# One trunk layer of a hybrid diffusion backbone: the ConvFFN's up projection with seven products of halves in place of eight

## The chip, the cores and the metric

The kernel runs on one core of a Trainium2 chip. The metric is the time of one execution in device microseconds (us). TensorE (PE) multiplies matrices and writes to PSUM, eight banks of 512 fp32 columns; VectorE (DVE), ScalarE (ACT) and GpSimd (POOL) work element by element, POOL on SBUF tiles only in this kernel; SyncE (SP) issues nearly all DMA transfers. Every engine takes its instructions in the order of its own queue, and semaphores hold an instruction until its operands and its buffer are ready.

## The reference

The layer takes a prompt of 128 tokens and 512 latent tokens, width 1,024, through norm, modulation, two kinds of attention and the ConvFFN, with a sandwich of norms around each. The change lies in the ConvFFN:

```python
def conv_ffn(h, w_up, conv_w, conv_b, w_down):
    u = h @ w_up
    up = jnp.pad(u, ((0, 0), (1, 1), (0, 0)))
    u = up[:, :-2] * conv_w[0] + up[:, 1:-1] * conv_w[1] + up[:, 2:] * conv_w[2] + conv_b
    gate, val = jnp.split(u, 2, axis=-1)
    return (jax.nn.silu(gate) * val) @ w_down
```

`w_up` is 1,024 x 5,632 (2,816 gate columns, then 2,816 value columns), `w_down` 2,816 x 1,024. Everything is fp32. The convolution runs along the tokens, over the 128 prompt tokens and the 512 latent ones apart.

## The kernel before

**Precision.** Every matrix product is made of three fp32r matmuls: each operand is split into a high part (a copy to fp32r on ScalarE, `act`, line 107) and a low part (the rest, a subtraction on VectorE, `tt`, line 110), and `mm3` (line 128) adds high x high, high x low and low x high into the same PSUM bank. `split` (121) does both steps for one tile.

**Units.** The 5,632 columns are cut into 22 units of 128 gate and 128 value columns (`NF`, line 20). `wtile` (532) loads one 1,024 x 128 block of weights (512 KB) as 8 blocks of 128 rows and splits it. The 640 tokens lie in `h2H` and `h2L` (two tiles each, four blocks of 128 channels per tile) with columns of zeros between the sequences, 644 columns in all (`TO`, 1291).

**Up.** For each unit, each of gate and value (`gv`) and each of two chunks of 322 and 324 token columns (`CH`, 1410), `up_mm` (1416) accumulates 8 x 3 = 24 matmuls into one bank: 96 matmuls for a unit. `up_ev` (1436) makes the convolution straight from the bank: a scaled copy with bias on ScalarE (middle tap), and two taps on VectorE (`stt`, line 118). `up_act` (1450) applies silu on ScalarE and multiplies gate by value on VectorE into `aT`, six SBUF tiles that hold all activations, 22 x 642 columns.

**What orders the work.** Up to line 1572 the order in each engine's queue is the order of the code (`manual_schedule`, from 1462; an earlier such region ends at line 1186). That part holds the out projection of attention, block by block of 128 tokens (`p_mm`, `p_y`, `p_sq`, `p_z`, `p_r`, `p_x`, `p_sx`, `p_n`, lines 1324 to 1356), the transposed and modulated input of the FFN (`p_T`, `p_h`, `p_s`, 1361 to 1390), the last modulation columns as filler for TensorE (`tick`, 1476, with loads `wms` on SP's queue), and the first chunk of units 0 and 1 (`up_mm(0, 0, 0)` to `up_ev(1, 1, 0)`, with weights `wu` split early). From 1573 on a scheduler at compile time orders the instructions; it may queue them ahead of hand-ordered ones.

**Down.** For each half of the 1,024 output columns, eleven steps (1622) load 256 rows of `w_down` (512 KB) and split them, split two units of `aT` into `aH` and `aL`, and add into five PSUM banks, one for each block of 128 tokens: 2 x 5 x 3 = 30 matmuls of 512 columns. `fin` (1606) closes a block with its norm and writes the output.

**Buffers.** SBUF tiles come from pools with a fixed number of buffers: `u` (10 large ones), `ws0` and `ws1` (one each, raw weights), `wh` and `wl` (two each, split weights), `pt` (6), `q` (2), `fp` (2), `p` (9). A tile waits until the last reader of the buffer's former tile is done.

## Time and profile before

| what | value |
|---|---|
| median of 3 runs | 869.59 us (866.78 to 872.27) |
| the profiled execution's own time | 876.65 us |
| span of its instructions | 874.9 us |
| up projection, units 2 to 21 | 428.7 to 714.8 us |
| down projection and output | 714.8 to 874.9 us |
| mean granted TensorE clock | 0.983 |

Times in rows of the profile are in us from the start of the span. A row of a group gives line, engine, operation, the tiles written and read (out<-in), their shapes and the count, then the busy time in us and the mean of one in ns, then the idle time of the engine just before these instructions and what ended it. A row of the timeline gives start and duration in us, and in brackets the idle time before. A row of the busy time by stretch gives for each engine the busy us and the count in that stretch, the granted clock, the DMA engines' mean busy share and GB/s. The line of an instruction is that of the helper that records it (107, 110, 119, 126), so tiles tell them apart.

### The profile page before, as it was taken

Reading aid. Unit: us, or ns where it says so; the run is one execution under the profiler, and the core shown is the slowest. Engines: PE = TensorE matmul, PEld = TensorE weight load, DVE = VectorE, ACT = ScalarE, POOL = GpSimd, SP = SyncE. Lnnn points to the kernel's source line nnn. Section 1 sums busy time; section 2 is a strip of 40 time slices with the busy share of each in tenths; the row PEclk is TensorE's granted clock in tenths of the full one; section 3 lists DMA queues with packets and bytes.
Section 4 is the critical chain, followed back from the end, with each engine's and each line's share of the span. In section 5 each row is a group of like instructions: output and inputs, shape, how many; then the busy total and the mean of one; then the engine's idle time right before and its main releaser. Section 6 shows DMA issues by size and latency. Waiting matters only on the chain.

```text
span 874.9 us, 14025 instructions
## 1 busy us (share of the span) xinstructions
PE 833.2 (95%) x5496; PEld 737.6 (84%) x5496; DVE 485.8 (56%) x1044; ACT 410.0 (47%) x829; POOL 129.9 (15%) x259
## 2 busy tenths in 40 slices
PE   2998999999999999999999999999999999999997
PEld 2767878888788778769999999999999998888885
DVE  1533556655788874577555555555555463427315
ACT  3433567645578885567433333333333352327112
POOL 1434143423231211142000000000000000000002
PEclk9989899999999998999999999999999999999999
DMA  6996555462622021644122222222222222222213
GB/s 134 256 246 110 142 145 145 117 172 76 151 73 72 27 73 37 208 146 121 49 73 73 73 73 73 73 73 76 80 83 76 73 71 75 73 72 73 85 60 120
DMA packets 136679, 88.09 MB, mean 101 GB/s; under 512 B 15753, under 2 KB 124581, under 8 KB 136613
## 3 DMA queue, kind: packets, MB, share of 16 engines
q1 hardware_dynamic: 135604, 86.54, 34.8%
q8 instruction: 43, 0.70, 0.3%
q10 hardware_dynamic: 1008, 0.66, 0.2%
q14 instruction: 24, 0.19, 0.1%
HBM read 83.16 MB, written 4.51 MB: 100 GB/s over the span
## 4 chain that ended last, share of the span: by engine, by line
PE 78%; DMA 7%; DVE 5%; ACT 5%; SPq 2%; issue 1%; POOL 1%; DVEq 0%; POOLq 0%; ACTq 0%
PE psu L126 36%; PE psd L126 18%; PE psg L126 9%; PE psya L126 3%; DMA wm<-in_w_mod_dram 2%; PE psS L126 2%; PE psO L126 2%; PE psyb L126 2%; ACT P L107 1%; PE psv L126 1%; PE psT L720 1%; DMA wms<-in_w_mod_dram 1%; DMA xs<-in_x_sample_dram 1%; PE psg L382 1%; SPq L233 1%
## 5 line engine op out<-in xcount | busy, mean ns | idle before, releaser
L126 PE MATMUL psu<-h2H,wh 128*128 128x322 f32 (+1 forms) x672 | 208.9, 311 | 0.0
L126 PE MATMUL psu<-h2H,wl 128*128 128x322 f32 (+1 forms) x672 | 208.8, 311 | 0.0
L126 PE MATMUL psu<-h2L,wh 128*128 128x322 f32 (+1 forms) x672 | 208.2, 310 | 0.0
L126 PEld LDWEIGHTS psu<-h2H,wh 128*128 128x128 f32 x672 | 127.1, 189 | 0.2 <-issue 0.2
L126 PEld LDWEIGHTS psu<-h2L,wh 128*128 128x128 f32 x672 | 127.0, 189 | 0.0
L126 PEld LDWEIGHTS psu<-h2H,wl 128*128 128x128 f32 x672 | 126.6, 188 | 0.0
L119 DVE SCALAR_TENSOR_TENSOR cv<-psu,T,cv 128x322 f32<-128x322 f32 (+1 forms) x176 | 96.6, 550 | 37.9 <-ACT cv L107 33.5
L107 ACT ACTIVATE wh<-wst 128x1024 fp32r<-128x1024 f32 x56 | 59.4, 1060 | 118.5 <-PE psu L126 55.2
L110 DVE TENSOR_TENSOR wl<-wst,wh 128x1024 fp32r<-128x1024 f32 (+1 forms) x45 | 54.6, 1214 | 101.4 <-ACT wh L107 101.2
L126 PE MATMUL psd<-wdl,aH 128*128 128x512 f32 x220 | 86.9, 395 | 0.0
L126 PE MATMUL psd<-wdh,aL 128*128 128x512 f32 x220 | 86.6, 394 | 0.0
L126 PE MATMUL psd<-wdh,aH 128*128 128x512 f32 x220 | 86.6, 394 | 0.0
L126 PE MATMUL psg<-hH,wh 128*128 128x320 f32 x224 | 77.4, 345 | 6.7 <-ACT T L107 3.1
L107 ACT ACTIVATE cv<-psu,T 128x320 f32<-128x320 f32 (+1 forms) x88 | 53.2, 607 | 45.5 <-PE psu L126 45.5
L126 PE MATMUL psg<-hH,wl 128*128 128x320 f32 x224 | 71.2, 318 | 0.0
L126 PE MATMUL psg<-hL,wh 128*128 128x320 f32 x224 | 71.2, 318 | 0.0
L116 POOL TENSOR_SCALAR rdv<-ssdc 128x1 f32<-128x1 f32 x5 | 1.9, 383 | 459.1 <-ACT jk L107 459.1
L126 PEld LDWEIGHTS psg<-hH,wh 128*128 128x128 f32 x224 | 44.0, 196 | 16.1 <-ACT T L107 7.0
L110 DVE TENSOR_TENSOR aL<-aT,aH 128x1284 fp32r<-128x1284 f32 x22 | 32.6, 1492 | 37.3 <-ACT aH L107 29.3
L110 DVE TENSOR_TENSOR wdl<-wd,wdh 128x1024 fp32r<-128x1024 f32 x22 | 26.9, 1222 | 47.2 <-ACT wdh L107 47.2
L107 ACT ACTIVATE wdh<-wd 128x1024 fp32r<-128x1024 f32 x22 | 23.2, 1055 | 61.2 <-PE psd L126 55.6
L126 PEld LDWEIGHTS psd<-wdl,aH 128*128 128x128 f32 x220 | 41.4, 188 | 9.9 <-DVE wdl L110 0.3
(277 smaller groups left out, 1513.5 us busy)
## 6 DMA issues: line engine op xcount, KB each, us to landing
wst<-in_w_up_dram SPq DMA_DIRECT2D x44, 512.0 KB
wms<-in_w_mod_dram SPq DMA_DIRECT2D x32, 512.0 KB
wd<-in_w_down_dram SPq DMA_DIRECT2D x22, 512.0 KB
...
```

The costliest lines, as they stand in the source:

```text
L107: return nc.scalar.activation(out=out, in_=in_, func=func, **kw)
L110: return (eng or nc.vector).tensor_tensor(out=out, in0=a, in1=b, op=op)
L116: return e.tensor_scalar(out=out, in0=a, scalar1=s1, scalar2=s2, op0=op0, op1=op1)
L119: return nc.vector.scalar_tensor_tensor(out=out, in0=a, scalar=s, in1=b, op0=op0, op1=op1)
L126: return nc.tensor.matmul(out, l, r, start=start, stop=stop, skip_group_check=True, **kw)
L233: nc.sync.dma_start(out=t[:, i], in_=wmod[:, o:o + 128].rearrange("(k p) f -> p k f", p=128))
L382: nc.tensor.matmul(ps_[32 * g:32 * g + 32, c0:c0 + n], cpad[:, k, :], chunks(k), start=(k < 4), stop=(k >= 4), tile_position=(0, 32 * g), ...
L720: nc.tensor.transpose(pst2[e][:, n * 128:n * 128 + 128], sf[e][0][:, o:o + 128], ident)
```

## The change

For units 2 to 21 the weights of a unit are seen as a matrix of halves, gate over value (`a1`, `a2`) by first and second half of the 1,024 channels, and the input as halves by channels and by tokens (`C1` and `C2`, 322 columns each). Seven products of halves, with sums of halves as operands, give the four results in place of eight. A product is 4 x 3 = 12 matmuls of 322 columns (`prod`), a unit 84 instead of 96.

- POOL makes the sums: once for the input (`p_e`, `t_sums`), and for each unit four of 128 x 512 for the weights (`sums`), into `b` (buffer `ws0`) and `a` (`ws1`). Four operands are split for a unit: `OA` (gate, 1,024 columns), `OSA` and `OSB` (sums, 1,024 each), `OC` (512): 3,584 columns where it was 2,048.
- The results leave PSUM in other ways: gate in two neighbouring banks (`ZX`), convolved whole (`tail_x`, 642 columns); value through copies and bank sums in an SBUF tile `VV` (`tail_v`). `unit` writes out the order of all queues; a unit's tail runs during the next unit, and the hand-ordered part now reaches to the end of unit 21.
- The input's unsplit halves `F` and `G` are kept (`hD` in DRAM for the first three blocks, read back by `fg_load`); units 0 and 1 keep the old products, but their results are copied to SBUF first and convolved later.
- The activations go to DRAM (`aD`, one store for each unit) and are read again in each half of the down projection (`ar`).
- The PSUM pools are closed and opened with other shapes before the second chunk of unit 0 and before the down projection; pool `u` has 11 buffers, `p` 8.

The diff, cut to its core:

```diff
+    PADS = (128, 641, 642, 643)
...
+    TO = [0, 129, 257, 385, 513]
+    HC = 322
+    C1, C2 = slice(0, HC), slice(HC, 2 * HC)
+    hD = dr_.tile([2, 128, 4, 644], F32, name="hD")
+    aD = dr_.tile([NF, 128, 642], F32, name="aD")
...
+    def p_e(t):
+        h0, h1 = (hfs[t, kb][1] for kb in range(2))
+        tt(h1, h1, h0, ALU.subtract, eng=nc.gpsimd)
+        if t < 3:
+            for kb, h_ in enumerate((h0, h1)):
+                nc.sync.dma_start(out=hD[kb, :, :, TO[t]:TO[t] + 128], in_=h_)
+    def fg_load():
+        for kb in range(2):
+            t_ = U([128, 4, 644], f"fg{kb}")
+            FG.append(t_)
+            for o in PADS:
+                nc.gpsimd.memset(t_[:, :, o:o + 1], 0.0)
+            for a, b in ((0, 128), (129, 385)):
+                nc.sync.dma_start(out=t_[:, :, a:b], in_=hD[kb, :, :, a:b])
...
+        act(raw[fi, gv][:, (C1, C2)[ch]], up.pop((fi, gv, ch)))
...
+    def conv_a(fi, gv, src):
+        fo = gv * NF + fi
         if fi not in cvs:
-            cvs[fi] = PT([128, 2, 642], "cv")
-        c0, n = CH[ch]
-        ps_ = up[fi, gv, ch] = PS("g" if (fi, gv, ch) == (1, 1, 0) else "gsot"[(2 * fi + gv) % 4], "psu")
-        side = ch == 1 and fi > 1
-        if side and sides:
-            side_load(None)
-            sd = side_gen(ps_[:, 324:454], PB([128, 128], "m2"), False)
-        for k in range(KD):
-            if side and k in (0, 3):
-                next(sd, None)
-            mm3(ps_[:, 0:n], wh[:, k, :], wl[:, k, :], h2H[k // 4][:, k % 4, c0:c0 + n],
-                h2L[k // 4][:, k % 4, c0:c0 + n], k == 0, k == KD - 1)
-        if side:
-            next(sd, None)
-            next(sd, None)
-
-    def up_ev(fi, gv, ch):
+            cvs[fi] = QT([128, 2, 642], "cv")
+        act(cvs[fi][:, gv], src[:, 0:642], ACTF.Identity, scale=T2[:, 44 + fo:45 + fo], bias=T2[:, 132 + fo:133 + fo])
+    def conv_d(fi, gv, src):
         fo = gv * NF + fi
-        w0, w1, w2, cb = (T2[:, i * 44 + fo:i * 44 + fo + 1] for i in range(4))
-        c0, n = CH[ch]
-        ps_ = up.pop((fi, gv, ch))
-        o_ = cvs[fi][:, gv, c0:c0 + n - 2]
-        act(o_, ps_[:, 1:n - 1], ACTF.Identity, scale=w1, bias=cb)
-        stt(o_, ps_[:, 0:n - 2], w0, o_, ALU.mult, ALU.add)
-        stt(o_, ps_[:, 2:n], w2, o_, ALU.mult, ALU.add)
-
-    def up_ch(fi, gv, ch):
-        up_mm(fi, gv, ch)
-        up_ev(fi, gv, ch)
-
...
+    def silu(fi):
+        act(cvs[fi][:, 0], cvs[fi][:, 0], ACTF.Silu)
+    def gate_mul(fi):
+        cv = cvs.pop(fi)
+        tt(cv[:, 0], cv[:, 0], cv[:, 1], ALU.mult)
+        nc.sync.dma_start(out=aD[fi], in_=cv[:, 0])
...
+            p_e(2)
+            fg_load()
...
+            p_e(t - 2)
...
+    psx.close()
...
+    pzx, pyy, pmm = pool2("pzx", 2), pool2("pyy", 2), pool2("pmm", 2)
+    ZS, XS = slice(512 - HC, 512), slice(512, 512 + HC)
...
+    def sums(u):
+        r = R[u]
+        a11, a12, a21, a22 = r[:, 0, 0:4], r[:, 0, 4:8], r[:, 1, 0:4], r[:, 1, 4:8]
+        b = SB[u] = WS([128, KD, 128], "sb", 0)
+        a = SA[u] = WS([128, KD, 128], "sa", 1)
+        g = nc.gpsimd
+        tt(b[:, 0:4], a21, a22, ALU.add, eng=g)
+        tt(a[:, 0:4], a11, a21, ALU.subtract, eng=g)
+        tt(a[:, 4:8], b[:, 0:4], a11, ALU.subtract, eng=g)
+        tt(b[:, 4:8], a12, a[:, 4:8], ALU.subtract, eng=g)
...
+    J = [(0, 191), (191, HC)]
+    def t_sums(j):
+        a, b = J[j]
+        p1, p2 = slice(a, b), slice(HC + a, HC + b)
+        g = nc.gpsimd
+        tt(F_[:, :, p2], F_[:, :, p2], F_[:, :, p1], ALU.subtract, eng=g)
+        tt(F_[:, :, p1], F_[:, :, p1], G_[:, :, p2], ALU.add, eng=g)
+        tt(G_[:, :, p1], G_[:, :, p1], G_[:, :, p2], ALU.subtract, eng=g)
+    def t_hl(t_, src, cs_):
+        act(t_[0][:, :, cs_], src[:, :, cs_])
+        tt(t_[1][:, :, cs_], src[:, :, cs_], f(t_[0][:, :, cs_]), ALU.subtract)
...
+    B11, B21, B22 = (h2H[0], h2L[0], C1), (h2H[1], h2L[1], C1), (h2H[1], h2L[1], C2)
+    T1_, T2_, T3_, T4_ = (*TF, C2), (*TF, C1), (*TG, C2), (*TG, C1)
+    def prod(out, o, k0, b, start=False):
+        for k in range(4):
+            mm3(out, o[0][:, k0 + k], o[1][:, k0 + k], b[0][:, k, b[2]], b[1][:, k, b[2]], start and k == 0, k == 3)
+    def tail_x(u):
+        src = ZX.pop(u)[:, 512 - HC:512 + HC]
+        conv_a(u, 0, src)
+        conv_d(u, 0, src)
+    def tail_v(u):
+        src = VV.pop(u)
+        conv_a(u, 1, src)
+        conv_d(u, 1, src)
+    def unit(u):
+        n, p = u + 1, u - 1
+        more, first = n < NF, u == 2
+        ZX[u] = zx()
+        YY[u] = pyy.tile([128, 512], F32, tag="y", name="yy")
+        VV[u] = FP([128, 644], "vv")
+        z, x, y = ZX[u][:, ZS], ZX[u][:, XS], YY[u][:, 0:HC]
+        prod(x, OA[u], 0, B11, True)
+        if not first:
+            tail_v(p)
+        act(z, x)
+        if more:
+            a_hi(n)
+            a_lo(n)
+        if not first:
+            prod(ZX[p][:, XS], OSB.pop(p), 4, B22)
+            tail_x(p)
+        sb_hi(u)
+        prod(y, OSA[u], 0, T3_, True)
+        act(VV[u][:, C2], y)
+        prod(x, OSA.pop(u), 4, T2_)
+        sb_lo(u)
+        if not first:
+            silu(p)
+            gate_mul(p)
+        act(VV[u][:, C1], x)
+        prod(y, OC.pop(u), 0, T4_)
+        if more:
+            sums(n)
+        prod(z, OA.pop(u), 4, B21)
+        tt(VV[u][:, C1], YY.pop(u)[:, 0:HC], VV[u][:, C1], ALU.add)
+        if more:
+            c_hi(n)
+            c_lo(n)
+            sa_hi(n)
+            sa_lo(n)
+        if u + 2 < NF:
+            r_load(u + 2)
+        prod(x, OSB[u], 0, T1_)
+        tt(VV[u][:, C2], x, VV[u][:, C2], ALU.add)
...
+    zz = [zx() for _ in range(2)]
+    for gv in range(2):
+        up_mm(0, gv, 1, zz[gv][:, ZS])
+    r_load(2)
+    t_sums(0)
+    t_hl(TG, G_, slice(HC, HC + 191))
+    t_sums(1)
+    for gv in range(2):
+        up_ev(0, gv, 1)
+    t_hl(TG, G_, slice(HC + 191, 2 * HC))
+    zz = [zx() for _ in range(2)]
+    for gv in range(2):
+        up_mm(1, gv, 1, zz[gv][:, ZS])
+    sums(2)
+    t_hl(TF, F_, C1)
+    t_hl(TG, G_, C1)
+    t_hl(TF, F_, C2)
+    a_hi(2)
+    a_lo(2)
+    sa_hi(2)
+    sa_lo(2)
+    c_hi(2)
+    c_lo(2)
+    for gv in range(2):
+        up_ev(1, gv, 1)
+    r_load(3)
+    for u in range(2):
+        for gv in range(2):
+            conv_a(u, gv, raw[u, gv])
+            conv_d(u, gv, raw[u, gv])
+        silu(u)
+        gate_mul(u)
+    for u in range(2, NF):
+        unit(u)
+        if u == 8:
+            gg2 = load_gate(S1, "ggb")
+    p = NF - 1
+    prod(ZX[p][:, XS], OSB.pop(p), 4, B22)
+    tail_v(p)
+    tail_x(p)
+    silu(p)
+    gate_mul(p)
+    psx.close()
+    pdd = pool2("pdd", 8)
     manual.close()
...
+            ar = (QT if half else PT)([128, 2, 642], "ar")
+            nc.sync.dma_start(out=ar, in_=aD[2 * kk:2 * kk + 2].rearrange("j p t -> p j t"))
+            split(ah[u][0][:, i2:i2 + 2, :], ah[u][1][:, i2:i2 + 2, :], ar)
```

More of the change, by code (lines that the diff above doesn't have):

```diff
@@ L22 @@
 NEG = -8e30
-NU = 10
+NU = 11
 @with_exitstack
@@ L1363, in p_T @@
             pt = PS("t", "psh2")
-            hfs[t, kb] = pt, PB([128, 512], "h2f")
+            if t > 2:
+                hf = FG[kb][:, :, TO[t]:TO[t] + 128]
+            else:
+                hf = PB([128, 512], "h2f").rearrange("p (k t) -> p k t", k=4)
+            hfs[t, kb] = pt, hf
             for kk in range(4):
@@ L1450, in up_act, with up_mm @@
-    def up_act(fi):
-        if fi % 4 == 0:
-            aT.append(U([128, 4, 642], f"aT{fi // 4}"))
-        cv = cvs[fi]
-        act(cv[:, 0], cv[:, 0], ACTF.Silu)
-        tt(aT[fi // 4][:, fi % 4, :], cv[:, 0], cv[:, 1], ALU.mult)
+    up = {}
+    raw = {}
+    def up_mm(fi, gv, ch, bank=None):
+        wh, wl = wu[fi, gv]
+        cs_ = (C1, C2)[ch]
+        if bank is None:
+            bank = PS("g" if (fi, gv, ch) == (1, 1, 0) else "gsot"[(2 * fi + gv) % 4], "psu")[:, 0:HC]
+        up[fi, gv, ch] = bank
+        for k in range(KD):
+            mm3(bank, wh[:, k, :], wl[:, k, :], h2H[k // 4][:, k % 4, cs_], h2L[k // 4][:, k % 4, cs_],
+                k == 0, k == KD - 1)
@@ L1559, in trunk_kernel @@
     p_s(3, 1, 1)
+    p_e(3)
     up_mm(1, 0, 0)
@@ L1591, in trunk_kernel, with pool2, zx @@
-    y0 = [y0t[t // 4][:, t % 4, :] for t in range(5)]
-    kinds = [["g", "g", "s", "s", "t"], ["t", "o", "o", "g", "g"]]
+    psx.close()
+    def pool2(name, bufs):
+        return psx.enter_context(
+            tc.tile_pool(name=name, bufs=bufs, space=bass.MemoryType.PSUM, reuse_waits="tile"))
+    pzx, pyy, pmm = pool2("pzx", 2), pool2("pyy", 2), pool2("pmm", 2)
+    ZS, XS = slice(512 - HC, 512), slice(512, 512 + HC)
+    def zx():
+        return pzx.tile([128, 1024], F32, tag="zx", name="zx")
@@ new lines, in wr2, with u2, hi, lo @@
+    def wr2(n):
+        return [wr_.tile([128, n, 128], F32R, tag=g_, name="o" + g_) for g_ in ("wh", "wl")]
+    def u2():
+        t_ = U([128, 2, KD, 128], "ou", F32R)
+        return t_[:, 0], t_[:, 1]
+    def hi(o, src):
+        act(o[0], src)
+    def lo(o, src):
+        tt(o[1], src, f(o[0]), ALU.subtract)
+    def a_hi(u):
+        OA[u] = u2()
+        hi(OA[u], R[u][:, 0])
+    def a_lo(u):
+        lo(OA[u], R[u][:, 0])
+    def c_hi(u):
+        OC[u] = wr2(4)
+        hi(OC[u], R[u][:, 1, 4:8])
@@ new lines, in c_lo, with sa_hi, sa_lo, sb_hi @@
+    def c_lo(u):
+        lo(OC[u], R[u][:, 1, 4:8])
+    def sa_hi(u):
+        OSA[u] = wr2(KD)
+        hi(OSA[u], SA[u])
+    def sa_lo(u):
+        lo(OSA[u], SA[u])
+    def sb_hi(u):
+        OSB[u] = u2()
+        hi(OSB[u], SB[u])
+    def sb_lo(u):
+        lo(OSB[u], SB[u])
+    F_, G_ = FG
+    TF = [U([128, 4, 644], f"tf{i}", F32R) for i in range(2)]
+    TG = [U([128, 4, 644], f"tg{i}", F32R) for i in range(2)]
+    J = [(0, 191), (191, HC)]
[6 more added lines that the diff above has]
+        tt(G_[:, :, p1], G_[:, :, p1], G_[:, :, p2], ALU.subtract, eng=g)
@@ L1596, in trunk_kernel @@
         fs = slice(half * 512, half * 512 + 512)
-        pd = [PS(kinds[half][t], f"psd{half}{t}") for t in range(5)]
+        pd = [pdd.tile([128, 512], F32, tag="d", name=f"psd{half}{t}") for t in range(5)]
         ah = {}
```

79 lines of the change are left out of this document (40 added, 39 removed).

## The prediction

> **What bounds the kernel now.** I read the page's head first, then the busy time by stretch of time, then the groups by form, then the timeline of a few places.
>
> ```profile
> span 874.9 us, 14025 instructions
> PE 833.2 (95%) x5496; PEld 737.6 (84%) x5496; DVE 485.8 (56%) x1044; ACT 410.0 (47%) x829; POOL 129.9 (15%) x259
> ```
> ```profile
> core 0: us, PE busy (x) PEld busy (x) DVE busy (x) ACT busy (x) POOL busy (x), PEclk, DMA share, GB/s
> 400.00:414.50 14.50, 14.50 (x116) 14.05 (x115) 10.71 (x18) 9.83 (x23) 3.23 (x5) 1.00 0.38 110
> 414.50:428.70 14.20, 14.20 (x98) 14.20 (x97) 10.06 (x16) 8.52 (x12) 0.00 (x0) 1.00 0.26 75
> 428.70:714.80 286.10, 286.07 (x1938) 285.67 (x1937) 150.63 (x222) 101.92 (x143) 0.00 (x0) 1.00 0.25 72
> 714.80:875.00 160.20, 153.68 (x662) 123.74 (x660) 71.36 (x66) 53.20 (x63) 4.73 (x10) 0.99 0.23 79
> ```
>
> The row 428.70:714.80 holds exactly the 20 units that the change touches: TensorE is busy for all of it at full granted clock, VectorE for half, ScalarE for a third, POOL not at all. One unit (gate and value, 2 x 48 matmuls) takes 286.1 / 20 = 14.3 us, a matmul 14.3 / 96 = 0.149 us. So TensorE's instruction stream is the bound here, and an eighth of it is worth 20 x 12 x 0.149 = 36 us if nothing else becomes the bound. The question is what the other engines then need per unit, in the order in which the new code queues them.
>
> **Durations for the new work.** The code adds no new kind of instruction, only other widths, so the groups of before price it.
>
> ```profile
> L107 ACT ACTIVATE wh<-wst 128x1024 fp32r<-128x1024 f32 x56 | 59.4, 1060 | 118.5 <-PE psu L126 55.2 <-issue 48.7 <-DMA wst<-in_w_in_dram 7.2
> L107 ACT ACTIVATE cv<-cv 128x642 f32<-128x642 f32 x22 | 16.3, 742 | 38.5 <-DVE cv L119 38.5
> L107 ACT ACTIVATE hH<-xnT,S,G 128x512 fp32r<-128x512 f32 x8 | 6.4, 801 | 0.0
> L110 DVE TENSOR_TENSOR wl<-wst,wh 128x1024 fp32r<-128x1024 f32 x44 | 53.9, 1226 | 101.2 <-ACT wh L107 101.2
> L119 DVE SCALAR_TENSOR_TENSOR cv<-psu,T,cv 128x322 f32<-128x322 f32 x88 | 48.4, 550 | 5.4 <-ACT cv L107 3.9
> L110 DVE TENSOR_TENSOR aT<-cv 128x642 f32<-128x642 f32 x22 | 18.2, 827 | 0.7
> L110 DVE TENSOR_TENSOR h2L<-h2f,h2H 128x512 fp32r<-128x512 f32 x10 | 6.9, 688 | 3.3 <-ACT h2H L107 3.3
> L110 DVE TENSOR_TENSOR q<-psg,q 128x320 fp32r<-128x320 f32 x8 | 3.9, 490 | 1.8 <-ACT q L107 1.8
> L119 DVE SCALAR_TENSOR_TENSOR Y<-y,rdr,Y 128x512 f32<-128x512 f32 x5 | 3.8, 752 | 1.7 <-POOL rdr L110 1.7
> L119 DVE SCALAR_TENSOR_TENSOR Y<-Y,ryr,xr 128x1024 f32<-128x1024 f32 x5 | 6.4, 1284 | 4.0 <-POOL ryr L110 4.0
> L110 POOL TENSOR_TENSOR wl<-wst,wh 128x1024 fp32r<-128x1024 f32 x11 | 26.7, 2423 | 52.4 <-ACT wh L107 39.0 <-PE pstb L972 11.6 <-PE psT L720 1.8
> ```
> ```profile
> 321.36 1.28 POOL L110 TENSOR_TENSOR ob<-o,ob 128x512 fp32r<-128x512 f32 x1 [15.66 <-ACT ob L107]
> 322.60 1.27 POOL L110 TENSOR_TENSOR cs<-cs,sqt 128x512 f32<-128x512 f32 x1
> ```
> ```profile
> 645.07 1.23 DVE L110 TENSOR_TENSOR wl<-wst,wh 128x1024 fp32r<-128x1024 f32 x1 [2.37 <-ACT wh L107]
> 646.21 1.13 DVE L119 SCALAR_TENSOR_TENSOR cv<-psu,T,cv 128x322 f32<-128x322 f32 x2
> ```
>
> Values: a high part of 1,024 columns 1.06 us on ScalarE, its low part 1.23 on VectorE (512 columns: 0.69); the silu 0.74; the gate product 0.83; adding a 322-column bank to an SBUF tile 0.49 (the 320-column row). The convolution's first tap on 642 columns lies between 0.80 (512 columns) and 1.00 (scaled by width); I take 0.90. A convolution tap on 641 columns lies between 0.75 and 1.28, by the line through both 0.89. A weight sum on POOL, 512 columns, takes 1.28, and two in a row start 1.24 apart. An independent VectorE instruction starts 0.09 before its forerunner's recorded end (645.07 + 1.23 against 646.21), a dependent pair takes 0.03 more than twice one (1.13 for two of 0.55). A hand-over between engines I take at 0.04.
>
> **The unit, by engine.** TensorE: 84 matmuls, 84 x 0.149 = 12.5 us. VectorE: low parts 3 x 1.23 + 0.69, four taps 3.56, two bank sums 0.98, gate product 0.83, together 9.7. POOL: four weight sums, 5.1. By sums alone TensorE stays the bound at 12.5.
>
> **The unit, as a loop.** But the order is written by hand, each queue is served in order, and one chain closes on itself once per unit. The sums for unit u+1 write the only `ws0` buffer, which holds `b` of unit u until its low part is taken. From there: three sums on POOL (3 x 1.28 less two overlaps of 0.04: 3.76); the high part of `sa` on ScalarE 1.06; its low part on VectorE 1.23; behind it in VectorE's queue the last bank sum of unit u 0.40; `tail_v` needs that sum: first tap on ScalarE 0.90, two taps on VectorE 1.80; behind them the low part of the next `OA` 1.14; behind that the two taps of `tail_x` 1.71; behind them the low part of `sb` for unit u+1, 1.14, and the loop is closed. Sum 13.1, with five hand-overs 13.3 us. That is already longer than TensorE's 12.5, so TensorE would wait.
>
> Two more VectorE instructions come into the loop if POOL and VectorE get in each other's way.
>
> ```profile
> 201.14 2.58 POOL L110 TENSOR_TENSOR wl<-wst,wh 128x1024 fp32r<-128x1024 f32 x1 [11.57 <-PE pstb L972]
> 201.39 2.48 DVE L110 TENSOR_TENSOR vb<-kx,vb 128x128 fp32r<-128x128 f32 x1
> ```
> ```profile
> L110 DVE TENSOR_TENSOR k<-cc,k 128x128 fp32r<-128x128 f32 x4 | 1.2, 301 | 0.4 <-ACT k L107 0.3
> ```
> ```profile
> 156.61 2.40 POOL L110 TENSOR_TENSOR wl<-wst,wh 128x1024 fp32r<-128x1024 f32 x1 [1.75 <-PE psT L720]
> ...
> 157.97 1.02 DVE L110 TENSOR_TENSOR ptL<-psT,ptH 128x384 fp32r<-128x384 f32 x2
> ```
>
> A subtraction of two SBUF tiles that takes 0.30 otherwise took 2.48 and ended with the POOL instruction that ran beside it; one with an operand in PSUM, `ptL`, ran beside POOL undisturbed (0.51 each). So a VectorE instruction with both tiles in SBUF and a POOL instruction exclude each other. The gate product of unit u-1 (0.83 - 0.09 = 0.74), queued right behind the low part of `sb`, then delays the first sum, and the low part of `c` (0.60) comes in between the sums: 13.3 + 1.3 = **14.6 us per unit**, against 14.3 before. The Trainium skill has the rule (page "SBUF — State Buffer", section "Who interferes with whom": a VectorE instruction with two SBUF inputs contends with a GpSimd instruction that reads SBUF, and the second one waits out the first). By that rule the loop is 14.6, without it 13.3; the trace agrees with it at 201.39. I take 14.6 with ends 13.3 (no exclusion) and 15.3 (the sums at 1.5 each). From unit 3 to unit 21 there are 18 such loops: 18 x (14.6 - 14.3) = **+5 us** (-18 to +18).
>
> **Ahead of the loop.** Removed there: 16 taps and 8 scaled copies of the first two units' half chunks, which lay beside TensorE. Added: `t_sums`, four splits of `TF` and `TG`, the sums and splits of unit 2. POOL: by the slope from 512 to 1,024 columns (1.28 to 2.42, 2.2 ns a column) 3 x 1.83 + 3 x 1.31 + 4 x 1.28 = 14.5 us. VectorE: low parts of 764, 524 and 3 x 1,288 columns at 1.05 ns a column plus 0.15, and those of unit 2, together 9.3. They exclude each other: 23.8 us in series, from about 2 us after the first halves' last matmul (414.5). TensorE has 14.2 us of `up_mm` for cover (row 414.50:428.70) and waits about 1 us ahead of it for the last old PSUM bank. ScalarE frees the bank that unit 2 wants only behind the high part of `sa`, at about 23.5: unit 2 starts 9 us late. Then `act(z, x)` of unit 2 is queued on ScalarE behind the whole convolution of units 0 and 1, and `cvs` of unit 1 waits for the store of unit 0 out of its buffer (two `q` buffers, one held by `raw1`): 0.9 + four taps 3.5 + 0.8 + store 3.2 + 0.9 + two taps 1.8 + 0.74, so `z` comes 12 us after unit 2's start, where in the loop it comes after 5.4. Less 1.3 for the tail that unit 2 doesn't have: 9 + 5.4 = **+15 us** (9 without the exclusion, 19 if the store is slow). The store's price is from the last output, 3.2 us from this instruction's end at 871.7 to the span's end:
>
> ```profile
> 870.95 0.74 DVE L119 SCALAR_TENSOR_TENSOR Y<-yb,rdr,Y 128x512 f32<-128x512 f32 x1
> ```
>
> **The first part of the FFN.** `p_e` puts five POOL subtractions, eight small memsets and six stores plus four loads on SP's queue between the norms.
>
> ```profile
> 401.07 0.73 POOL L116 TENSOR_SCALAR ryv<-ssy 128x1 f32<-128x1 f32 x1
> ...
> 403.69 1.22 DVE L110 TENSOR_TENSOR wu<-wst,wu 128x1024 fp32r<-128x1024 f32 x1
> ```
> ```profile
> L735 POOL MEMSET ptH<- 64x128 f32 x16 | 3.6, 224 | 4.5 <-DVE ptL L110 4.4
> ```
> ```profile
> 406.47 0.40 PE L126 MATMUL psu<-h2H,wu 128*128 128x322 f32 x1
> ```
>
> The statistic of the last block at 401.07 now stands behind `p_e(2)` (1.28) and the memsets (8 x 0.22 = 1.8): 3.1 us, and `wu`, which ends at 404.91 and is wanted at 406.47, comes late by the other 1.5. **+2 us** (0 if covered; 8 if SP's stores, each waiting for POOL, hold up the modulation weights behind them, since TensorE runs without a gap there, row 400.00:414.50).
>
> **The end.** The seventh product of unit 21 runs after its unit, and two of the five first banks of the down stage are freed only by `tail_x`: 0.9 + 1.8 us, of which six matmuls of 153.68 / 662 = 0.23 us cover 1.4. Loads for the down stage need not wait behind the last store: SP issued loads of the free part ahead of one of the hand-ordered part before.
>
> ```profile
> 88.17 0.53 SPq L833 DMA_DIRECT2D wms<-in_w_mod_dram  x1
> 88.76 2.92 SPq L265 DMA_DIRECT2D traw<-ftab  x4
> 97.91 0.37 SPq L349 DMA_DIRECT2D wst<-in_w_in_dram  x1
> ```
>
> (88.17 and 88.76 follow line 1186, 97.91 stands before it.) **+2 us** (0 to 14, the latter if load and splits follow the last store). In the down stage each of 22 steps of 30 matmuls (6.9 us) now also loads 0.66 MB beside 0.52: 170 GB/s. The page's line shows slices above 200, so I take it as hidden; at 146 a step would be 8.1 us and cost up to 26 us in all.
>
> ```profile
> GB/s 134 256 246 110 142 145 145 117 172 76 151 73 72 27 73 37 208 146 121 49 73 73 73 73 73 73 73 76 80 83 76 73 71 75 73 72 73 85 60 120
> ```
>
> Sum: 2 + 15 + 5 + 2 = **+24 us**. The profiled execution took 876.65 (span 874.9 and 1.75 around it): 901 for it. The shown runs have a median 7 us lower, 869.59: forecast **893 us**.
>
> **Rivals.**
> 1. *The exclusion doesn't act on these instructions, or seldom.* The loop is 13.3, the start costs 9: 2 + 9 - 18 + 2 = -5, 865 us, no change. For it: most POOL instructions before had little beside them. Against: the rows above. Chance 0.2.
> 2. *TensorE stays the bound*, because the order leaves more room than I see (say the bank sum doesn't wait for the low part of `sa`): 12.5 per unit, 18 x (12.5 - 14.3) = -32; 2 + 9 - 32 + 2 = -19, 850 us, faster. It decides once the loop is under 13.0. For it: VectorE's sum of 9.7 and ScalarE's third. Against: two engines must be wrong by a whole microsecond in a loop of ten terms. Chance 0.18.
> 3. *The reload in the down stage is not hidden*, or the sums are slowed to 1.5 by VectorE's turns: at 15.3 per unit 893 + 13 = 906, with a step of 8.1 us 893 + 26 = 919. Chance 0.17.
>
> My forecast has 0.45. About 1% is what a measurement of this kernel tells from no change. Faster by more: 0.19 (rival 2 and a little of 1). Within 1%, 861 to 878: 0.21 (the rest of rival 1 and the lowest edge of the forecast). Slower: 0.60. The range takes in rival 1 and most of 3, and leaves the lower half of rival 2 and the extreme of 3: 854 to 910; the forecast's own range is 880 to 906.
>
> **What would show it.** Right: TensorE's busy share in the unit stretch falls to about 85%, with waits of `P1` to `P4` products on VectorE low parts and ScalarE copies; a unit lasts 14.6; VectorE's low parts of 512 and 1,024 columns and the gate product are stretched beside POOL's sums; a gap of some 9 us in TensorE before `act(z, x)` of unit 2. Wrong: units of 12.5 with TensorE at 99%; POOL sums ending well before the low part of `sa` is wanted; waits of the down stage on DMA.

## The result, and where the time went

The changed kernel takes 904.54 us (median of 4 runs, 901.37 to 911.58) against 870.93 us for the kernel before in the same runs (866.78 to 873.79): 1.040 times, with a 95% interval of 1.033 to 1.048. It is slower by 33.6 us, where the prediction had +24 and gave a slower kernel 0.60.

The profiled execution took 911.58 us, 34.9 more than that of before (876.65). First the head of its page, then its busy time by stretch; the columns of the stretches are those of the prediction's first table.

```profile
span 909.5 us, 13912 instructions
PE 819.0 (90%) x5256; PEld 714.3 (79%) x5256; DVE 543.7 (60%) x1045; ACT 458.5 (50%) x898; POOL 270.3 (30%) x358
```
```profile
384.50:400.00 15.50, 11.94 (x85) 9.17 (x85) 7.13 (x18) 6.30 (x16) 4.28 (x4) 0.78 0.80 223
418.90:439.60 20.70, 14.54 (x97) 14.22 (x96) 12.28 (x8) 9.74 (x16) 19.62 (x11) 0.97 0.24 65
439.60:461.20 21.60, 14.79 (x72) 14.51 (x73) 14.42 (x16) 10.34 (x16) 4.83 (x5) 0.71 0.27 79
461.20:723.20 262.00, 236.92 (x1531) 232.24 (x1530) 178.17 (x200) 127.30 (x182) 107.89 (x72) 0.97 0.34 94
740.40:783.60 43.20, 38.85 (x151) 30.09 (x151) 24.92 (x20) 21.32 (x19) 0.00 (x0) 0.92 0.74 244
```

TensorE's work fell from 833.2 to 819.0 us: by 14 us and not by the 36 of an eighth of the units, since the granted clock was lower in places. Its share fell from 95% to 90%, because the time outside its work (span less busy time) grew from 41.7 to 90.5 us. Both have their source at four places. The row 461.20:723.20 is the 18 units from the first product of unit 3 to the first product of unit 21, TensorE busy for 90% of it. The row 439.60:461.20 is unit 2, at a granted clock of 0.71. The row 740.40:783.60 is the beginning of the down projection: 151 matmuls where 43.2 us held 187 before.

From the two traces, by marks that both have (last `psst` matmul of attention, end of the first chunks of units 0 and 1, first product of unit 3 and of unit 21, first and last `psd` matmul), in us:

| part | before | after | difference | predicted |
|---|---|---|---|---|
| attention and before | 347.9 | 344.2 | -3.7 | 0 |
| first part of the FFN | 66.6 | 74.8 | +8.2 | +2 |
| start of the units, to unit 3 | 28.5 | 42.3 | +13.8 | +15 |
| 18 units | 257.7 | 261.9 | +4.2 | +5 |
| unit 21 to the down projection | 14.2 | 17.2 | +3.0 | +2 |
| down projection | 153.6 | 162.5 | +8.9 | 0 |
| output | 6.4 | 6.7 | +0.3 | 0 |

They sum to +34.7. Each column is one execution, and both were longer than the medians of their kernels, by 6 and 7 us. The first line is not the change's doing in any way that was found: over the kernels of this study, which differ later, it varied from 336.2 to 344.8. For that reason single runs are compared below by these parts and not by their whole time.

**The loop of the units.** This is the timeline of VectorE, ScalarE and POOL for one unit of the changed kernel, from one first sum to the next (instructions that lie beside the chain left out).

```profile
690.06 0.82 DVE L111 TENSOR_TENSOR cv<-cv 128x642 f32<-128x642 f32 x1
690.23 1.81 POOL L111 TENSOR_TENSOR sb<-wraw 128x512 f32<-128x512 f32 x1 [8.37 <-DVE ou L111]
...
692.00 1.29 POOL L111 TENSOR_TENSOR sa<-wraw 128x512 f32<-128x512 f32 x1
...
692.84 1.00 DVE L111 TENSOR_TENSOR owl<-wraw,owh 128x512 fp32r<-128x512 f32 x1
693.25 1.73 POOL L111 TENSOR_TENSOR sa<-sb,wraw 128x512 f32<-128x512 f32 x1
695.02 1.06 ACT L108 ACTIVATE owh<-sa 128x1024 fp32r<-128x1024 f32 x1 [3.48 <-POOL sa L111]
...
696.11 1.33 DVE L111 TENSOR_TENSOR owl<-sa,owh 128x1024 fp32r<-128x1024 f32 x1 [2.27 <-ACT owh L108]
697.36 0.48 DVE L111 TENSOR_TENSOR vv<-zx,vv 128x322 f32<-128x322 f32 x1
697.87 0.92 ACT L108 ACTIVATE cv<-vv,T 128x642 f32<-128x642 f32 x1 [1.80 <-DVE vv L111]
...
698.83 1.81 DVE L120 SCALAR_TENSOR_TENSOR cv<-vv,T,cv 128x641 f32<-128x641 f32 x2 [0.99 <-ACT cv L108]
...
700.55 1.22 DVE L111 TENSOR_TENSOR ou<-wraw,ou 128x1024 fp32r<-128x1024 f32 x1
...
701.69 1.80 DVE L120 SCALAR_TENSOR_TENSOR cv<-zx,T,cv 128x641 f32<-128x641 f32 x2
...
703.41 1.22 DVE L111 TENSOR_TENSOR ou<-sb,ou 128x1024 fp32r<-128x1024 f32 x1
```

The next first sum starts at 704.70: 14.47 us after 690.23. From start to start: three sums 4.79, high part of `sa` 1.09, its low part 1.25, bank sum 0.51, first tap 0.96, two taps 1.72, low part of `OA` 1.14, two taps 1.72, low part of `sb` 1.29. Every link of the predicted chain is there, in its order. Where VectorE and POOL meet, both are late: the first sum lasts 1.81 behind the gate product, the third 1.73 behind the low part of `c`, which itself takes 1.00 where 0.69 was its price.

**The first part of the FFN.** SP's queue, then TensorE and POOL, in the timeline of the changed kernel.

```profile
375.97 6.98 SPq L1407 DMA_DIRECT2D hD<-h2f  x2
383.05 0.57 SPq L1502 DMA_DIRECT2D wms<-in_w_mod_dram  x1
...
388.06 1.08 PE L383 MATMUL psada<-wms,cpad 128*32 128x128 f32 x16 [3.48 <-DMA wms<-in_w_mod_dram]
...
403.77 1.74 POOL L111 TENSOR_TENSOR h2f<-h2f 128x512 f32<-128x512 f32 x1
...
405.45 0.33 POOL L1414 MEMSET fg<- 128x4 f32 x8
405.74 0.30 POOL L117 TENSOR_SCALAR ryv<-ssy 128x1 f32<-128x1 f32 x1
...
409.42 0.38 PE L848 MATMUL psada<-sel,m 128*128 128x2 f32 x2 [1.31 <-ACT m L108]
```

Two stores keep SP for 6.98 us, since the second waits for POOL's subtraction; the modulation weights are issued behind them, and TensorE waits 3.48 us. The statistic `ryv` comes behind POOL's subtraction (1.74) and memsets, and TensorE waits 1.31 a second time. The rest of the 8.2 us is in the granted clock (third number from the end), here in the busy time by stretches of 2 us:

```profile
386.00:388.00 2.00, 0.00 (x0) 0.00 (x0) 1.28 (x3) 0.71 (x2) 1.50 (x2) 0.84 0.96 310
390.00:392.00 2.00, 2.00 (x6) 1.52 (x5) 0.15 (x1) 0.00 (x0) 1.28 (x1) 0.50 0.82 235
396.00:398.00 2.00, 1.92 (x24) 1.49 (x25) 0.09 (x1) 1.97 (x6) 0.00 (x0) 1.00 0.38 105
```

After the wait TensorE is granted 0.50 until about 394 and the full clock only from 396. The Trainium skill (page "TensorE: Matmul & The Clock Gate", section "Part 1: The HAM clock gate") says that the array falls to half its clock after an idle window of about 3.4 us and comes back after about as long of sustained work. The trace agrees here in kind, with some 6 us at 0.50 behind a wait of 3.48; the last section shows falls behind shorter waits, which this rule does not cover.

**The start of the units.** ScalarE's queue ahead of `act(z, x)` of unit 2 (the last row):

```profile
439.20 0.75 ACT L108 ACTIVATE raw<-zx 128x322 f32<-128x322 f32 x2
439.84 1.73 ACT L108 ACTIVATE cv<-raw,T 128x642 f32<-128x642 f32 x2
...
448.82 1.74 ACT L108 ACTIVATE cv<-raw,T 128x642 f32<-128x642 f32 x2 [3.41 <-DMA aD<-cv]
...
452.33 0.42 ACT L108 ACTIVATE zx<-zx 128x322 f32<-128x322 f32 x1
```

TensorE waits 5.22 us (434.45 to 439.67) for the bank that the copies at 439.20 free, and 6.74 us (446.06 to 452.80) for the copy at 452.33, which stands behind the convolutions of units 0 and 1 and the store between them. The 72 matmuls of unit 2 would take 72 x 0.149 = 10.7 us at full clock; the row 439.60:461.20 shows 14.79 busy at 0.71, so 4.1 us went to the clock.

**The down projection.** Its first eight steps are 7.02, 7.82, 9.99, 11.37, 7.08, 6.99, 7.00 and 7.06 us long, where all took 6.9 to 7.0 before. ScalarE's queue in the third:

```profile
757.00 1.28 ACT L108 ACTIVATE aH<-ar 128x1284 fp32r<-128x1284 f32 x1 [1.84 <-DMA ar<-aD]
762.92 1.28 ACT L108 ACTIVATE aH<-ar 128x1284 fp32r<-128x1284 f32 x1 [4.64 <-DMA ar<-aD]
764.11 1.04 ACT L108 ACTIVATE wdh<-wd 128x1024 fp32r<-128x1024 f32 x1
```

The split of the next weights at 764.11 stands behind two splits of `ar`, each of which waits for its DMA. TensorE waits for `wdh` and `wdl` only 4.4 us in all, and between 766 and 772 it is again granted 0.50 to 0.56.

### The profile page after: what moved, and what is told of

Same layout as the page of the kernel before. It is cut to its first block, busy times and chain, and to the rows that moved or that the text cites. A ratio compares the mean times of both kernels' runs of the same rounds, so it can differ in the third digit from the quotient of the medians.

```text
span 909.5 us, 13912 instructions
## 1 busy us (share of the span) xinstructions
PE 819.0 (90%) x5256; PEld 714.3 (79%) x5256; DVE 543.7 (60%) x1045; ACT 458.5 (50%) x898; POOL 270.3 (30%) x358
## 4 chain that ended last, share of the span: by engine, by line
PE 37%; DVE 18%; POOL 13%; DMA 11%; ACT 10%; issue 7%; SPq 2%; DVEq 0%; POOLq 0%; ACTq 0%
PE psd L127 15%; PE psg L127 8%; POOL sa L111 7%; DVE cv L120 6%; DVE ou L111 5%; POOL sb L111 4%; PE psya L127 3%; DMA wm<-in_w_mod_dram 2%; ACT owh L108 2%; PE psyb L127 2%; ACT cv L108 2%; PE psS L127 2%; DMA ar<-aD 2%; DMA scr<-rpx 2%; PE psO L127 2%
## 5 line engine op out<-in xcount | busy, mean ns | idle before, releaser
L127 PE MATMUL zx<-h2H,ou 128*128 128x322 f32 x480 | 121.7, 322 | 30.9 <-DVE vv L111 25.7
L127 PEld LDWEIGHTS zx<-h2H,ou 128*128 128x128 f32 x480 | 85.7, 194 | 36.1 <-DVE vv L111 30.6
L111 POOL TENSOR_TENSOR sb<-wraw 128x512 f32<-128x512 f32 x20 | 36.4, 1821 | 169.5 <-DVE ou L111 169.5
L127 PE MATMUL zx<-h2L,ou 128*128 128x322 f32 x240 | 76.0, 317 | 0.0
L127 PE MATMUL yy<-tg,owh 128*128 128x322 f32 x320 | 75.9, 324 | 0.0
L111 DVE TENSOR_TENSOR owl<-sa,owh 128x1024 fp32r<-128x1024 f32 x20 | 27.4, 1368 | 59.5 <-ACT owh L108 59.5
L127 PEld LDWEIGHTS yy<-tg,owh 128*128 128x128 f32 x320 | 58.2, 203 | 0.1
L111 DVE TENSOR_TENSOR aL<-ar,aH 128x1284 fp32r<-128x1284 f32 x22 | 32.9, 1494 | 35.4 <-PE psd L127 18.4
L127 PEld LDWEIGHTS psd<-wdh,aH 128*128 128x128 f32 x220 | 42.0, 191 | 12.9 <-ACT wdh L108 3.0
L127 PE MATMUL yy<-tg,owl 128*128 128x322 f32 x160 | 51.8, 324 | 0.0
```

The costliest lines, as they stand in the source:

```text
L111: return (eng or nc.vector).tensor_tensor(out=out, in0=a, in1=b, op=op)
L127: return nc.tensor.matmul(out, l, r, start=start, stop=stop, skip_group_check=True, **kw)
```

## The experiments

Eleven kernels were run. The parts of each, in us, by the marks of the table above:

| kernel | first part | start of units | 18 units | to down | down | whole time |
|---|---|---|---|---|---|---|
| before | 66.6 | 28.5 | 257.7 | 14.2 | 153.6 | 869 to 873 |
| after | 74.8 | 42.3 | 261.9 | 17.2 | 162.5 | 904.54 |
| e1_order | 73.1 | 43.7 | 229.1 | 16.1 | 156.3 | 870.11 |
| e2_sums_dve | 73.5 | 41.1 | 227.8 | 15.3 | 159.0 | 861.04 |
| e3_no_gate | 74.2 | 43.6 | 251.9 | 19.6 | 157.5 | 897.89 |
| e4_no_reload | 73.5 | 43.5 | 260.6 | 18.7 | 155.7 | 905.12 |
| e5_stores | 69.5 | 43.3 | 262.5 | 15.7 | 161.3 | 901.18 |
| e6_prolog | 74.1 | 33.0 | 268.0 | 18.6 | 158.4 | 897.23 |
| e7_down | 73.9 | 43.5 | 260.5 | 24.6 | 158.8 | 909.71 |
| e8_all | 70.2 | 34.4 | 237.1 | 21.3 | 159.3 | 872.9 |
| e10_best | 70.8 | 28.1 | 238.5 | 15.1 | 156.0 | 861.14 |
| e11_dve_all | 70.5 | 43.3 | 226.8 | 15.1 | 156.0 | 862.93 |
| e12_dve_sums | 69.8 | 27.6 | 234.3 | 15.1 | 155.8 | 855.95 |

**1. The same work in another order.** The parts of `sb`, whose low part frees `ws0` for the next sums, go to the start of the unit, and the split of the next `OA` behind its fourth product.

```diff
+        sb_hi(u)
+        sb_lo(u)
         prod(x, OA[u], 0, B11, True)
...
         act(z, x)
+        if not first:
+            prod(ZX[p][:, XS], OSB.pop(p), 4, B22)
+            tail_x(p)
+        prod(y, OSA[u], 0, T3_, True)
+        act(VV[u][:, C2], y)
+        prod(x, OSA.pop(u), 4, T2_)
         if more:
             a_hi(n)
             a_lo(n)
-        if not first:
-            prod(ZX[p][:, XS], OSB.pop(p), 4, B22)
-            tail_x(p)
-        sb_hi(u)
-        prod(y, OSA[u], 0, T3_, True)
-        act(VV[u][:, C2], y)
-        prod(x, OSA.pop(u), 4, T2_)
-        sb_lo(u)
```

> Same work, other order: the high and low part of sb of unit u are taken at the start of unit u, ahead of both tails of unit u-1, and the splits of the next OA at its end. So the low part of sb, which frees the only ws0 buffer for POOL's next sums, no longer stands behind the bank sum, tail_v, the OA low part and tail_x: the loop is cut. Theory (the loop of sums, sa parts, bank sum, tails, sb parts sets 14.5 us a unit): units of 12.4 to 12.7 us with TensorE above 97% busy in that stretch, 18 x 1.8 to 2.1 = 32 to 38 us less, about 868. Rival (TensorE itself, or the throughput of VectorE and POOL with their mutual exclusion, needs 14.5 a unit): units stay at 14.5, about 904.

870.11 us (10 runs), 1.002 times the kernel before (0.999 to 1.005). The unit is 12.45 us. Here are the busy time in the stretch of the 18 units and two groups in it:

```profile
456.10:685.20 229.10, 227.72 (x1530) 225.91 (x1529) 205.77 (x201) 130.29 (x183) 120.28 (x72) 1.00 0.39 108
```
```profile
L111 POOL TENSOR_TENSOR sa<-sb,wraw 128x512 f32<-128x512 f32 x18 | 35.0, 1947 | 0.0
L111 DVE TENSOR_TENSOR cv<-cv 128x642 f32<-128x642 f32 x18 | 34.5, 1914 | 0.0
```

TensorE is busy for 99%, with not one instruction less on VectorE or POOL. The two engines even hinder each other more than before: the gate product lasts 1.91 instead of 0.82, the third sum 1.95. It costs nothing, since neither is on the chain any more. So the 14.5 us was the loop, and neither TensorE nor the amount of work on VectorE and POOL. The 18 units take 229.1 us instead of 257.7 before the change: 28.6 less, of the 32 (18 x 12 x 0.149) that an eighth of the products is worth. So one reordering makes the whole loss of 34 us good, but it does not remove it where it arose: the first part and the start of the units stay as slow as they were.

**2. The sums on VectorE.**

```diff
-        g = nc.gpsimd
+        g = nc.vector
```

> The four weight sums of every unit are made by VectorE (0.69 us each by the nearest row) instead of POOL (1.28 each by the row, 1.8 for the last one in this trace); order unchanged. Nothing runs on POOL in the units, so nothing can exclude VectorE. Theory (loop, with exclusion as part of it): three sums 2.0 instead of 3.8 in the loop, no stretched instructions, units of 12.5 to 13.3, 21 to 36 us less. Rival (POOL only lies beside the loop, or TensorE is the bound at 14.5): no change, or longer because VectorE now has 12 us of work a unit.

One run: 861.04 us, the 18 units 227.8. Their busy time by stretch:

```profile
450.70:678.50 227.80, 227.11 (x1530) 226.10 (x1529) 207.11 (x271) 128.92 (x182) 0.00 (x0) 1.00 0.39 108
```

VectorE now has 70 instructions more, but is busy for 207.11 us, against 205.77 in experiment 1 with the sums on POOL: what the sums take on VectorE, POOL's sums had cost it in stretched instructions. The low part of `c`, 1.22 us on average in the changed kernel's units, is at its own price in this kernel's groups over the same stretch:

```profile
L111 DVE TENSOR_TENSOR owl<-wraw,owh 128x512 fp32r<-128x512 f32 x18 | 12.3, 681 | 0.0
```

A second cut through the same loop, with the order unchanged, gives the same unit of 12.5. The start of the units, 41.1 us, gains little: experiments 3, 4, 5 and 7, which leave it as it was, have 43.3 to 43.6, the changed kernel 42.3.

**3. No gate product.**

```diff
-        tt(cv[:, 0], cv[:, 0], cv[:, 1], ALU.mult)
+        if fi < 2:
+            tt(cv[:, 0], cv[:, 0], cv[:, 1], ALU.mult)
```

> The product gate x value of units 2 to 21 is left out (VectorE, two SBUF operands, 0.83 us); the store is kept and writes the gate alone. By dependences the product is not in the loop. If POOL's sum and a VectorE instruction on two SBUF tiles exclude each other, the first sum, queued behind the low part of sb, now starts some 0.74 us sooner and the units take 13.7 instead of 14.5: 13 us less, about 891. If they do not exclude each other, units stay at 14.5.

A unit takes 13.97 us (14.47 with the product), so 0.5 less where 0.74 was expected, and the 18 units 251.9. No operand of the chain comes from this product; it is in the loop only because POOL's first sum cannot run beside it. The page's group of the first sum shows it: 1.36 on average, where it was 1.82 in the changed kernel.

```profile
L111 POOL TENSOR_TENSOR sb<-wraw 128x512 f32<-128x512 f32 x20 | 27.2, 1358 | 169.7 <-DVE ou L111 169.7
```

**4. No reload in the down projection.**

```diff
-            ar = (QT if half else PT)([128, 2, 642], "ar")
-            nc.sync.dma_start(out=ar, in_=aD[2 * kk:2 * kk + 2].rearrange("j p t -> p j t"))
+            if kk == 0:
+                ar = (QT if half else PT)([128, 2, 642], "ar")
+                nc.sync.dma_start(out=ar, in_=aD[2 * kk:2 * kk + 2].rearrange("j p t -> p j t"))
```

> The down projection loads the activations ar once for each half and uses that tile for all its steps; the other loads of ar are left out. Theory (the reload of ar on SP's queue ahead of the down weights makes the first steps of the down stage 7.8, 10.0 and 11.4 us long instead of 7.0): all steps 7.0, about 9 us less, about 895. Rival (those steps wait for PSUM banks, the tail or the splits of the weights): they stay long, no change.

This kernel leaves out all loads of `ar` but the first of each half. The down projection takes 155.7 instead of 162.5 us; all steps are 7.0 but the third, 8.39, and no split waits for an `ar` there. So the steps of 10 and 11 us go with the waits behind the reload. How much of the 8.9 us these are is not shown: experiments 1, 2, 3, 5 and 6 have the same down projection as the changed kernel, and take between 156.3 and 161.3 in their single profiles. The whole time of this one run, 905.12, doesn't show the gain: other parts differ by as much between runs.

**5. The stores at the end of the round.** The stores of `hD` are issued after the round's modulation weights, and `p_e(2)` with `fg_load` after the last block's statistic.

```diff
-        if t < 3:
-            for kb, h_ in enumerate((h0, h1)):
-                nc.sync.dma_start(out=hD[kb, :, :, TO[t]:TO[t] + 128], in_=h_)
+    def p_st(t):
+        for kb in range(2):
+            nc.sync.dma_start(out=hD[kb, :, :, TO[t]:TO[t] + 128], in_=hfs[t, kb][1])
...
+        if 1 < t < 4:
+            p_st(t - 2)
```

> First part of the FFN alone: the stores of the first two blocks go onto SP's queue at the end of their round instead of ahead of the next modulation weights, and the subtraction, the memsets and the reload of the third block's tile come behind the last block's statistic. Same work. Theory (SP's queue stands 6.98 us behind stores that wait for POOL, TensorE waits 3.48 us for the modulation weights and then runs at a granted clock of 0.50 for some 6.5 us; the statistic late by the memsets costs 1.3): the part from the last psst matmul to the end of the first chunks takes 67 to 69 us instead of 74.8, so 6 to 8 us less, about 897. Rival (the added DMA traffic and POOL time themselves cost it, wherever they are queued): 74 us, no change.

The part takes 69.5 us, 5.3 less. The same stores now hold SP for 1.56 us, TensorE's waits for `wms` are 1.11 and 0.36, the one for the statistic is 0.64, and its busy time in a stretch as long as 384.50:400.00 shows the full clock:

```profile
380.60:396.10 15.50, 13.93 (x126) 11.46 (x127) 10.38 (x20) 8.43 (x22) 7.70 (x9) 1.00 0.96 212
```

The DMA engines moved about as much (212 GB/s against 223), so it was the place in the queue. Of the 2.9 us that remain against before, 1.8 are in these three waits, where before had one of 0.33; the rest is unexplained.

**6. Another order at the start of the units.** `sums(2)` ahead of the tile sums on POOL, `up_ev(1, gv, 1)` ahead of the late splits, and the convolutions of units 0 and 1 moved into unit 2; the splits of unit 2's operands come earlier as well.

```diff
     r_load(2)
+    sums(2)
+    p_e(4)
     t_sums(0)
...
-    for u in range(2):
-        for gv in range(2):
-            conv_a(u, gv, raw[u, gv])
-            conv_d(u, gv, raw[u, gv])
-        silu(u)
-        gate_mul(u)
```

> Start of the units alone: POOL makes the weight sums of unit 2 ahead of the tile sums, ScalarE frees the second pair of banks ahead of the late splits, and the convolution of units 0 and 1 goes behind act(z, x) of unit 2 (its VV is put in another pool's tile, since the raw tiles are still in use). Same work. Theory (the 14 us there are the order of ScalarE's queue: 5.22 us for the old bank, 6.74 us for act(z, x) behind the convolution, and a granted clock of 0.72 after both): the stretch from the end of the first chunks to the first product of unit 3 falls from 42.3 to 28 to 32 us, 10 to 14 less, about 893. Rival (POOL and VectorE exclude each other for 24 us of work, whatever the order): 38 to 42 us, at most 4 less.

The start of the units falls from 42.3 to 33.0, as the theory has it, but unit 3 then takes 18.7 instead of 13.2 us, and the 18 units together 6.1 more: net 3 less. The waits at the start were the order of ScalarE's queue, but the convolutions' some 9 us of VectorE work (eight taps of 0.88, two gate products of 0.82) only came later, into a loop that had no room. The theory is right on the place and the rival on the net gain.

**7. The down projection in an order written by hand.** Loads four steps ahead, splits two steps ahead, weights ahead of `ar`.

```diff
+            d_prep(s_ + 2)
+            if s_ + 4 < 22:
+                d_load(s_ + 4)
```

> Down projection alone: its order is written by hand too (loads four steps ahead, splits two steps ahead, for each step the weights ahead of the reloaded activations) instead of left to the scheduler, which put up to three splits of ar ahead of the next weights' split on ScalarE. Same work and the same reload. Theory (ScalarE and VectorE stand behind an ar that has not landed while the weights lie ready): all steps 7.0, the stage 154 to 157 instead of 162.5 us, 6 to 9 less, about 897. Rival (the reload's 0.66 MB a step beside 0.52 is more than the DMA brings): steps of 7.8 and more stay, or every step is a little longer.

The time, 909.71, is no better, and the reason is a new wait. But the steps are what the theory asked for. First its busy time by stretch (the first step, then about six more), then a line of TensorE's waits (us in total, times, longest):

```profile
742.30:751.60 9.30, 8.99 (x31) 6.78 (x32) 3.99 (x4) 2.03 (x2) 0.00 (x0) 0.77 0.84 267
751.60:794.80 43.20, 43.20 (x186) 34.80 (x185) 15.99 (x12) 14.28 (x13) 0.00 (x0) 1.00 0.51 164
```
```profile
PE psd L127 <- ACT aH L108: 5.8, 1, 5.8
```

With the full reload, from the second step on TensorE is busy without a gap at 164 GB/s: 186 matmuls in 43.2 us, as before. So the reload is hidden by bandwidth; it was not hidden by the order of ScalarE's queue. What spoils this run is that its first splits are queued behind the last unit's tail: TensorE waits 5.76 us, and the first step lasts 9.30 at a clock of 0.77.

**8. All four edits** (1, 5, 6 and 7 together).

> The four edits together: sb's parts at the start of a unit, the stores at the end of the round, the sums and convolutions at the start of the units, and the down projection by hand. If the four causes are separate places on the path that sets the end, their gains add: 904.5 - 34 - 7 - 12 - 8 = 843, about 0.97 of the kernel before (faster by 3%). Rival (a gain in one stage is taken back in the next, or the clock is granted less over longer busy time): 855 to 870, no faster than before.

872.9 us, 1.003 times before (1.001 to 1.006). The gains did not add: edit 7's wait of 5.76 us is in it, and the start of the units with unit 3 takes 34.4 + 20.7 = 55.1 us, where edit 1 alone has 43.7 + 12.5 = 56.2.

**9. The four edits mended.** The first splits of the down projection go into the last unit, its first five banks are ones that the tail doesn't hold, unit 2's sums are VectorE's, and `sb`'s parts and the split of `TF`'s second half come behind `act(z, x)` of unit 2. The convolution of unit 1 now lies in unit 3, ahead of the value tail of unit 2, and `sums(2)` goes back behind the first tile sums.

```diff
-        g = nc.gpsimd
+        g = nc.vector if u == 2 else nc.gpsimd
...
+        if not more:
+            d_hi(0)
         prod(x, OSB[u], 0, T1_)
```

> All four edits again, two of them mended by what the run with all four showed: the down projection's first splits go ahead of the last unit's tail and its first five banks are ones that the tail does not hold (there TensorE waited 5.76 us), unit 2's sums go to VectorE, and sb's parts and the late split of the tile sums come behind act(z, x) of unit 2 on ScalarE (5.84 us). Theory (these two waits were queue order): from 872.9 about 5.8 + 3 less for the down stage with its first step at full clock, and 5 to 8 less at the start of the units: 856 to 859, some 1.3% under the kernel before. Rival (POOL's tile sums, VectorE's splits and the convolutions of units 0 and 1 are too much work for the start of the units in any order): 864 to 868, no difference from before.

861.14 us, 0.987 times before (0.983 to 0.991). The wait of 5.76 us is gone. The start of the units is at 28.1 us, what it was before the change, but unit 3 takes 21.97.

**10. All sums on VectorE, start of the units left as it was.** Edits 1, 5 and the mended 7.

```diff
-        g = nc.gpsimd
+        g = nc.vector
```

> All weight sums on VectorE, sb's parts at the start of the unit, the stores at the end of the round and the mended down projection; the start of the units stays as in the changed kernel but for VectorE's sums. Theory (gains in separate stages add): one run with the sums on VectorE took 861; 5 less in the first part of the FFN, 4 to 6 less in the down projection: 850 to 853, some 2% under the kernel before. Rival (12.5 us of VectorE work a unit is as long as TensorE's 12.5, so any disturbance is not made good): 858 to 865.

862.93 us, 0.989 (0.983 to 0.996): the rival's range. The units are 12.45 us but for unit 8 (15.07, long in every kernel), so VectorE with all the sums does not become the bound; the missing 10 us are in parts that the edits were not to lengthen: by the traces, against the run that took 861, attention is 8 us longer and the start of the units 2, and the first part gave 3 of the expected 5.

**11. The ninth kernel with all sums on VectorE.**

```diff
-        g = nc.vector if u == 2 else nc.gpsimd
+        g = nc.vector
```

> The version with the four edits mended (861.14), but with all weight sums on VectorE. There unit 3 took 21.97 us: four taps of a convolution, 3.52 alone, lasted 6.40 beside POOL's sums. Theory (a POOL sum and a VectorE instruction on SBUF tiles take turns, so four sums of 1.28 to 1.9 on POOL take more of VectorE's time than four of 0.69 on VectorE itself): the taps are 3.5 again, unit 3 takes 17 to 19 us, all later units 12.45, and the whole is 4 to 6 us less, 855 to 857, some 1.7% under the kernel before. Rival (POOL's sums are work taken off VectorE): VectorE has 2.8 us more to do a unit, the start of the units gets longer and later units cannot make it good: 862 or more.

855.95 us (6 runs), 0.981 times before (0.978 to 0.983), the best here. The taps of the two moved convolutions, from 430 to 460 us, in the ninth kernel (the group, then each convolution in the timeline) and in this one (the group):

```profile
L120 DVE SCALAR_TENSOR_TENSOR cv<-raw,T,cv 128x641 f32<-128x641 f32 x8 | 9.8, 1244 | 1.0 <-ACT cv L108 0.9
437.72 6.40 DVE L120 SCALAR_TENSOR_TENSOR cv<-raw,T,cv 128x641 f32<-128x641 f32 x4
451.59 3.53 DVE L120 SCALAR_TENSOR_TENSOR cv<-raw,T,cv 128x641 f32<-128x641 f32 x4 [0.85 <-ACT cv L108]
```
```profile
L120 DVE SCALAR_TENSOR_TENSOR cv<-raw,T,cv 128x641 f32<-128x641 f32 x8 | 6.9, 884 | 0.1
```

The four taps at 437.72 lie beside POOL's sums and take 1.60 each, the four at 451.59 do not and take 0.88. Unit 3 falls from 21.97 to 18.70 us. So at the start of the units, taking work off VectorE to POOL had cost VectorE more than it saved: four sums on POOL are 5.1 us and more that exclude VectorE's instructions on two SBUF tiles, four on VectorE are 2.7. In the later units it makes no difference (12.45 in experiment 1 too).

## Why the prediction was right, and where it was wrong

**The loop: right, in mechanism and size.** Predicted 14.6 us a unit, measured 14.47; +5 predicted for 18 units, +4.2 measured. The chain's terms are each within 0.15 us of the steps measured above, but for the sums with their exclusion (5.10 against 4.79), so this is not luck. TensorE's share in the stretch is 90% and not the 85% that was named as a sign, in part because its clock is lower there (0.97). Experiments 1 and 2 cut the loop at two different links, and both times TensorE became the bound at 12.45 (predicted 12.5 by sums alone). So rival 2's unit of 12.5 exists, but not in this order.

**The exclusion: right, a little over-priced.** Without it the loop was put at 13.3. Experiment 3 shows the gate product worth 0.5 instead of 0.74. The Trainium skill's rule (page "SBUF — State Buffer", section "Who interferes with whom") is borne out by the sums and low parts that are stretched only side by side: 1.00 against 0.68 for the low part of `c`, 1.81 against 1.36 for the first sum. Rival 1 is refuted.

**Ahead of the loop: the sum right in part by luck.** +15 (its terms add up to 14.4) against +13.8. Unit 2 starts 6.5 us late, where +9 was predicted: 20.7 us behind the first chunks, 14.2 before. And it lasts 21.6 us, 7.4 more than before, where +5.4 was predicted. The two errors nearly cancel. The waits that were named are there, 5.22 and 6.74 us, but the granted clock, which took 4.1 us of unit 2, is in no term. The first mechanism was priced as work in series; experiment 6 shows that the place of the work can be changed, and experiments 6, 8 and 9 that it then comes back in unit 3.

**The first part of the FFN: the step that was mis-sized.** It was put at +2, and 8 was named for the case that SP's stores hold up the modulation weights. That case happened: +8.2. So the mechanism and its price were on the page, but the sum took the other branch: the queue was not followed to the second store of a block, which waits for POOL's subtraction ahead of weights that TensorE has no cover for. The delay that the +2 stood for was over-priced (eight memsets at 1.8 us; the row at 405.45 has 0.33 for all). Experiment 5 takes back 5.3 by moving the stores.

**The down projection: the step that failed.** "I take it as hidden" was right for the bytes, as experiment 7 shows, and wrong for the stage: +8.9 in the changed kernel's profile, 2.7 to 7.7 in the five others with the same down projection. The sign of being wrong that was named, waits of the down stage on DMA, is in the rows of ScalarE. Rival 3 priced the same reload by bandwidth (steps of 8.1 to the end, up to 26). Instead the first steps alone were slow, because a scheduler had put splits of tiles that were still on their way ahead of splits that TensorE needed next. The prediction looked at the DMA engines and not at the queue that stands behind them.

**The end: the size near, the term another.** +2 against +3.0. The wait for banks of the tail, which was predicted, is not there: the first step of the down projection takes 7.02 us, 7.04 before. Unit 21 takes 15.3 us, 14.2 before, and its seventh product adds 1.9.

**What no term has** is the granted clock behind a wait. In the first part 4.8 us of waits go with a loss of 8.2, at the start of the down projection 4.4 with 8.9. These two misses, together 15 us, are why the changed kernel took 904.54 us and not the forecast's 893; the attention part, shorter by 3.7, hides some of it.

**Left open:** the shorter attention part of the changed kernels (3 to 12 us in single profiles), the rest of the first part, the size of the reload's share in the down projection, and which waits make the clock fall.
